# Three sample-token products with 128 columns of weights in a delta-rule decoder kernel

## The chip, the cores and the metric

One core of a Trainium2 chip runs the whole kernel in one launch. The metric is the device time of an execution in microseconds; the time of a kernel is the median of its runs.

## The reference, cut to what matters

The reference is one inference step of a hybrid decoder layer with 1088 tokens of 1024 features: 1024 tokens of a new sequence (the prompt) and 64 sample tokens, 8 sequences of 8 tokens each, that continue from stored states. One input projection gives the inputs of a pooling branch and of a gated delta branch with 8 heads of 128. The delta branch, for each head and each chunk of tokens, computes

```
u = w_v - w_k @ s            # w_v, w_k: solutions of a unit triangular system
o = qg @ s + (q @ k.T * decay) @ u
s = glast * s + kt.T @ u
```

For the prompt this runs over chunks with a state `s` that is carried on; for the sample tokens each sequence is one chunk of 8 with its own starting state `s0`. All 64 sample tokens of a head fit in one 64x64 matrix that is block-diagonal with blocks of 8. The change touches only products of these 64 sample tokens. After the branches come two output projections (`pa`, `pb`), a merge by gates, a last projection (`wo`) and a layer norm.

## The kernel before, in words

All big projections ("dense") have a weight tile of 128 output features as the stationary side and 1088 tokens, in column chunks of 364, 362 and 362, as the moving side. Each fp32 weight and activation is split into a high and a low part in fp32r (`wh`, `wl`, `hhi`, `hlo`), so that one output chunk is 24 matmuls. ScalarE makes `wh`, GpSimd subtracts it from the raw weight for `wl` (`wsplit`, line 336), a tile ahead of its use. The small fp32 products of the delta branch are single calls in the code that show as two passes each in the profile ("x2").

The order of instructions is written out by a planner inside the kernel. The main generator (`phaseD`, line 1731) yields after each dense matmul; helper generators (`aux`) wait for flags, or for estimated times, and put their instructions between the dense matmuls. `_Timed.g` (line 140) keeps an estimated clock of each engine: a GpSimd operation with two inputs costs 0.17 + n/400 us, another one 0.17 + n/1050; a TensorE fp32 product costs n/550 us, a third of it when the output has 32 partitions, and half when it has 64 and n is 64. `bank("m", x, ...)` (line 290) lets a helper go on when TensorE's estimated time has reached the estimated completion of its inputs and of the last use of one of two PSUM banks. The estimate knows when an input was written; of the reuse of a buffer it knows nothing. On the chip every engine runs its own instructions in this order and waits on semaphores.

The delta phase runs for each head `h` three dense tiles (Q, V, ZB) in the main generator and, between them, these helpers:

- `pre` and `prep` (line 1459). `prep` copies the sample columns of key and query into `kq` on GpSimd, multiplies `kt.T @ q` for eight prompt chunks of 128 tokens, then for the 64 sample tokens: `kt[:, TP:T]`, 128 rows by 64 columns, is the stationary side, 64 query columns are the moving side. VectorE multiplies the result by the decay in `e2`.
- `recur` (line 1495), the chain over eight chunks of the prompt, with products between `S`, `ktr`, `ttm`, `r`, `uh`, `qg`.
- `samples` (line 1550). Sixteen narrow products with `s0` (32 weight columns each), two VectorE steps that give `r` (tile `rs_`), then two products with the inverse `tt[:, TP:T]`, 64 columns, once for partitions 0 to 63 of the result and once for 64 to 127 (so the result `u` stands twice); ScalarE copies `u` and its high part, GpSimd the low part and the spread form `ux`; then four products of 32 columns and 64 rows with `pt` (tile `e2r`), each for 16 tokens, the 16 columns ahead of them being of no use; a transpose, and the new states.
- `vtoks` (line 1695) copies the sample part of `v` twice into `v2` on GpSimd and transposes it on TensorE.
- `post0`, `post1` (line 1651), the head norm; the last step issues the store to `d_yb`.

In the phase behind it (`phaseD7`, line 1795) `pa` tiles are computed until the flag of head 7's `post1` is set at the end of one; then buffers are exchanged and `yb` is loaded and split for the `pb` tiles.

In the profile all instructions have line L163, the one line of the helper that issues them, so groups are told apart by tile names: `psm<-us,e2r`, `psm<-rs_...,ttm` and `psm<-q,ktr` with 64 columns are the products that the change touches.

Of the kernel before, what the change touches and what calls it, by code (L numbers as in the profile page):

```python
# [9 lines left out]
F32 = mybir.dt.float32  # L10
# [8 lines left out]
TP = 1024  # L19
NB = 8  # L20
TS = 64
T = TP + TS
# [193 lines left out]
class _K:  # L216
# [1128 lines left out]
        self.flush()  # L1345


    def s128(self, nm):
        return self.X.tile([128, 128], F32, tag="u", name=nm, bufs=12)

    def loads(self, h):
        nc = self.nc
# [37 lines left out]
    def loads3(self, h):  # L1390
        nc, L = self.nc, self.L[h]
        L["s0"] = self.t("s0", shape=(128, 8, 128))
        nc.sync.dma_start(out=L["s0"], in_=self.A["s0"][h])

    def bc(self, ap, h, c0, n, p0, p1, w):
        return ap[p0:p1, c0:c0 + n, h].unsqueeze(2).to_broadcast([p1 - p0, n, w])
# [62 lines left out]
    def prep(self, h):  # L1459
        nc = self.nc  # L1460
        L = self.L[h]
        q = L["q"] = self.q[h]
        kt, e2 = L["kt"], L["e2"]
        kq = L["kq"] = self.s128("kq")
        gx = lambda ap: ap.rearrange("p (g x i) -> p g x i", x=2, i=16)
        gi = lambda ap: ap[:, TP:T].rearrange("p (g i) -> p g i", i=16)
        for x, src in enumerate((kt, q)):
            nc.gpsimd.tensor_copy(gx(kq)[:, :, x, :], gi(src))
        qg = L["qg"]

        def scaled():
            yield from self.on(qg)
            for i in range(4):
                cs = slice(256 * i, 256 * i + 256)
                nc.gpsimd.tensor_tensor(out=qg[:, cs], in0=qg[:, cs], in1=q[:, cs], op=ALU.mult)
                yield 3
            self.flags.add(("qg", h))
        self.aux(scaled())
        for g in range(2):
            ps = yield from self.bank("m", kt, q, e2)  # L1480
            for c in range(4):
                cs = slice(128 * (4 * g + c), 128 * (4 * g + c) + 128)
                nc.tensor.matmul(ps[:, 128 * c:128 * c + 128], kt[:, cs], q[:, cs], start=True, stop=True)
            gs = slice(512 * g, 512 * g + 512)
            nc.vector.tensor_tensor(out=e2[:, gs], in0=ps, in1=e2[:, gs], op=ALU.mult)
        ps = yield from self.bank("m")
        nc.tensor.matmul(ps[0:64, 0:64], kt[:, TP:T], q[:, TP:T], start=True, stop=True)
        nc.vector.tensor_tensor(out=e2[0:64, TP:T], in0=ps[0:64, 0:64], in1=e2[0:64, TP:T], op=ALU.mult)
        yield from self.until(("qg", h))
        for c0, n in CHUNKS:  # L1490
            cs = slice(c0, c0 + n)
            nc.scalar.activation(out=q[:, cs], in_=q[:, cs], func=AF.Square, scale=(RMS_EPS * 128.0) ** 0.5)
            yield 3
# [56 lines left out]
    def samples(self, h):  # L1550


        nc = self.nc
        V = nc.vector
        L = self.L[h]
        s0, kq, o, pt = L["s0"], L["kq"], L["qg"], L["e2"]
        ps = yield from self.bank("m", kq, s0)
        for j in range(2):
            for g in range(4):
                nc.tensor.matmul(ps[32 * g:32 * g + 32, 128 * j:128 * j + 128], kq[:, 32 * g:32 * g + 32],  # L1560
                                 s0[:, 2 * g + j, :], start=True, stop=True)
        r, u = self.s128("rs_"), self.s128("us")
        V.scalar_tensor_tensor(out=r, in0=ps[:, 0:128], scalar=self.cg[:, 0, h:h + 1], in1=L["vs"],
                               op0=ALU.mult, op1=ALU.add)
        V.scalar_tensor_tensor(out=r, in0=ps[:, 128:256], scalar=self.cg[:, 1, h:h + 1], in1=r,
                               op0=ALU.mult, op1=ALU.add)
        ps = yield from self.bank("m", r, L["tt"])
        for p0 in (0, 64):
            nc.tensor.matmul(ps[p0:p0 + 64, 0:128], L["tt"][:, TP:T], r, start=True, stop=True)
        self.acopy(u, ps[:, 0:128])  # L1570
        uh = self.X.tile([128, 128], F32R, tag="u", name="ush", bufs=12)
        ul = self.X.tile([128, 128], F32R, tag="u", name="usl", bufs=12)
        self.acopy(uh, u)
        nc.gpsimd.tensor_tensor(out=ul, in0=u, in1=uh.bitcast(F32), op=ALU.subtract)

        def spread(half):
            x = self.t("ux", F32R, (128, 2, 4, 128))
            for i, w in enumerate((uh, ul)):
                nc.gpsimd.tensor_tensor(
                    out=x[:, i], in0=w.bitcast(F32).unsqueeze(1).to_broadcast([128, 4, 128]),  # L1580
                    in1=self.cst[:, C_BM + 4 * half:C_BM + 4 * half + 4].unsqueeze(2)
                    .to_broadcast([128, 4, 128]), op=ALU.mult)
            return x
        ux = spread(0)
        ps = yield from self.bank("m", u, pt)
        for g in range(4):
            c0 = TP + 16 * g - 16
            nc.tensor.matmul(ps[32 * g:32 * g + 32, 0:128], pt[0:64, c0:c0 + 32], u[0:64],
                             start=True, stop=True)
        ot = self.s128("ot")  # L1590
        V.tensor_tensor(out=ot, in0=ps[:, 0:128], in1=r, op=ALU.add)
        ps = yield from self.bank("m", ot)
        nc.tensor.transpose(ps[:, 0:128], ot, self.ident)
        V.tensor_copy(o[:, TP:T].rearrange("p (g i) -> p g i", i=16),
                      ps[:, 0:128].rearrange("p (g x i) -> p g x i", x=2, i=16)[:, :, 1, :])
        self.aux(self.osq(L, slice(TP, T)))
        for half in range(2):
            ps = yield from self.bank("m", L["ks"], ux)
            for i in range(2):
                nc.tensor.matmul(ps, L["ks"], ux[:, i].rearrange("p b e -> p (b e)"),  # L1600
                                 start=(i == 0), stop=(i == 1))
            if half == 0:
                x1 = spread(1)
            for b in range(4):
                bb = 4 * half + b
                yield from self.free(4.0)
                V.scalar_tensor_tensor(out=s0[:, bb, :], in0=s0[:, bb, :], scalar=self.gls[:, bb, h:h + 1],
                                       in1=ps[:, 128 * b:128 * b + 128], op0=ALU.mult, op1=ALU.add)
                yield 1
            if half == 0:  # L1610
                ux = x1
        yield from self.on(s0)
        self.store(self.A["o_ds"][h], s0)
# [427 lines left out]
```

## Time and profile before

| | |
|---|---|
| median of 3 runs | 1293.39 us (1293.36 to 1293.54) |
| profiled execution | 1293.13 us |
| its span, first to last instruction | 1291.4 us |
| TensorE matmul (PE) busy | 1272.5 us, 99%, 8216 instructions |
| TensorE weight load (PEld) busy | 1215.8 us, 94%, 8216 |
| VectorE (DVE) | 796.1 us, 62%, 1383 |
| ScalarE (ACT) | 545.1 us, 42%, 1288 |
| GpSimd (POOL) | 640.0 us, 50%, 869 |

The profiled execution is 1.7 us longer than its span, which is the time around the first and the last instruction. Busy shares are averages over the whole span. A matmul's end is modelled and overlaps the start of the next, so the time that TensorE spends on an instruction is read from one start to the next, not from the durations. Timeline rows merge instructions of one kind that follow each other; a row of `x4` begins at the first one's start and lasts to the last one's end.

### The profile page before, as it was taken

To read this page: it belongs to the slowest core of one execution; us is meant where nothing else is said; L and a number is where in the kernel's file an instruction comes from. 1 tells how busy PE (TensorE), PEld (TensorE's weight loads), DVE (VectorE), ACT (ScalarE), POOL (GpSimd) and SP (SyncE) were. 2 spreads that over 40 slices of the span, in tenths; PEclk is the share of its full clock that TensorE was granted. 3 is DMA by queue.
4 is the path that set the end of the run, shared out by engine and by line. 5 is a ranking of instruction groups with operands and counts; after the bars stand their busy time and mean duration, and the time that the engine had idled before them with its cause. 6 is when DMAs were issued, how large, how long until landed. Compare 5 with 4: busy or idle time off the path is not lost. (4 is left out here: it accounts for less than half of the span.)

```text
span 1291.4 us, 21998 instructions
## 1 busy us (share of the span) xinstructions
PE 1272.5 (99%) x8216; PEld 1215.8 (94%) x8216; DVE 796.1 (62%) x1383; ACT 545.1 (42%) x1288; POOL 640.0 (50%) x869
## 2 busy tenths in 40 slices
PE   7999999999999999999999999999999999999996
PEld 5899999999999999999999999999999999999885
DVE  4465567899915999725656567565567443443367
ACT  3576685432354224443545455354464232231011
POOL 4446566644647457434555553554549422253124
PEclk9999999999999999999999999999999999999999
DMA  9334574424264222264332324323353385455123
GB/s 374 132 133 144 183 229 144 129 93 146 101 197 140 85 95 75 75 199 138 99 127 75 101 77 156 120 61 120 122 189 125 125 261 195 139 177 179 66 103 110
DMA packets 112746, 178.79 MB, mean 138 GB/s; under 512 B 57584, under 2 KB 76544, under 8 KB 111616
## 3 DMA queue, kind: packets, MB, share of 16 engines
q1 hardware_dynamic: 111424, 173.02, 41.2%
q0 software_dynamic: 736, 4.21, 1.2%
q8 instruction: 65, 1.06, 0.4%
q14 instruction: 41, 0.34, 0.1%
q10 hardware_dynamic: 480, 0.16, 0.1%
HBM read 127.69 MB, written 49.65 MB: 137 GB/s over the span
## 5 line engine op out<-in xcount | busy, mean ns | idle before, releaser
L163 PE MATMUL psd<-hlo,wh 128*128 128x364 f32 x1488 | 494.7, 332 | 0.0
L163 PE MATMUL psd<-hhi,wl 128*128 128x364 f32 x1488 | 494.6, 332 | 0.0
L163 PE MATMUL psd<-hhi,wh 128*128 128x364 f32 x1488 | 494.5, 332 | 0.0
L163 POOL TENSOR_TENSOR wl<-wr,wh 128x256 fp32r<-128x256 f32 x328 | 289.8, 895 | 349.1 <-ACT wh L163 337.2
L163 PEld LDWEIGHTS psd<-hhi,wh 128*128 128x128 f32 x1488 | 280.6, 189 | 3.2 <-issue 1.7
L163 PEld LDWEIGHTS psd<-hlo,wh 128*128 128x128 f32 x1488 | 280.9, 189 | 2.1 <-issue 1.3
L163 PEld LDWEIGHTS psd<-hhi,wl 128*128 128x128 f32 x1488 | 280.7, 189 | 1.8 <-issue 1.2
L163 DVE SCALAR_TENSOR_TENSOR cacc<-cext,small,cacc 128x362 f32<-128x362 f32 (+2 forms) x216 | 153.4, 722 | 67.6 <-ACT cacc L163 63.2
L163 ACT ACTIVATE wh<-wr 128x256 fp32r<-128x256 f32 x328 | 122.7, 407 | 28.2 <-PE psd L163 17.7
L163 DVE TENSOR_TENSOR P<-Tm,L 128x2048 f32<-128x2048 f32 (+35 forms) x136 | 111.5, 820 | 4.6
L163 DVE TENSOR_REDUCE Tm<-P 128x64 f32<-128x2048 f32 (+38 forms) x136 | 87.6, 644 | 4.2
L163 ACT ACT_TABLE_LOAD x65 | 83.4, 1283 | 5.5 <-issue 2.4
L163 ACT ACTIVATE cext<-psd 128x364 f32<-128x364 f32 (+1 forms) x88 | 32.4, 394 | 83.1 <-PE psd L163 83.0
L163 POOL TENSOR_TENSOR q<-q,o 128x128 f32<-128x128 f32 (+1 forms) x72 | 33.6, 468 | 67.8 <-ACT o L163 64.2
L163 PE MATMUL psd<-yah,wh 128*128 128x362 f32 (+1 forms) x192 | 63.8, 332 | 0.0
L163 PE MATMUL psd<-yah,wl 128*128 128x362 f32 (+1 forms) x192 | 63.4, 330 | 0.0
L163 PE MATMUL psd<-yal,wh 128*128 128x362 f32 (+1 forms) x192 | 63.3, 330 | 0.0
L163 PE MATMUL psd<-ybh,wh 128*128 128x362 f32 (+1 forms) x192 | 63.0, 328 | 0.0
L163 PE MATMUL psd<-ybl,wh 128*128 128x362 f32 (+1 forms) x192 | 63.0, 328 | 0.0
L163 PE MATMUL psd<-ybh,wl 128*128 128x362 f32 (+1 forms) x192 | 62.6, 326 | 0.0
L163 ACT ACTIVATE sz<-psd 128x362 f32<-128x362 f32 (+1 forms) x48 | 22.5, 473 | 90.6 <-PE psd L163 90.6
L163 ACT ACTIVATE sg<-psd 128x362 f32<-128x362 f32 (+1 forms) x48 | 22.8, 474 | 83.7 <-PE psd L163 83.6
(290 smaller groups left out, 2203.5 us busy)
## 6 DMA issues: line engine op xcount, KB each, us to landing
wr<-win SPq DMA_DIRECT2D x64, 512.0 KB
wada<-wada SPq DMA_DIRECT2D x16, 512.0 KB
gcb<-d_gc SPq DMA_DIRECT2D x8, 576.0 KB
xt<-xT SPq DMA_DIRECT2D x8, 544.0 KB
d_ga<-sg SPq DMA_DIRECT2D x8, 544.0 KB
d_e<-e SPq DMA_DIRECT2D x8, 544.0 KB
d_k<-kt SPq DMA_DIRECT2D x8, 544.0 KB
d_ya<-ya SPq DMA_DIRECT2D x8, 544.0 KB
```

The source lines that it names most:

```text
L163: return f(*a, **kw)
```

## The change

One buffer of 128x128 (`w2`) is added, and three products get 128 columns of weights. In `prep`, GpSimd copies `kt[:, TP:T]` twice side by side into `kd`, and the product gives its 64 rows twice. In `samples`, GpSimd copies `tt[:, TP:T]` twice side by side into `td`, and one product gives what two gave. Then GpSimd clears `w`, copies the 64x64 sample part of `pt` into every second group of 16 columns of its upper half, and one product takes the place of four. `kd`, `td` and `w` use the one buffer in turn. The waits (`bank`) name the copies.

```diff
-    def s128(self, nm):
-        return self.X.tile([128, 128], F32, tag="u", name=nm, bufs=12)
+    def s128(self, nm, tag="u", bufs=12):
+        return self.X.tile([128, 128], F32, tag=tag, name=nm, bufs=bufs)
...
+    def twice(self, copy, out, in_):
+
+        copy(out.rearrange("p (a i) -> p a i", a=2), in_.unsqueeze(1).to_broadcast([128, 2, 64]))
...
         self.aux(scaled())
+        kd = self.s128("kd", "w2", 1)
+        self.twice(nc.gpsimd.tensor_copy, kd, kt[:, TP:T])
         for g in range(2):
...
-        ps = yield from self.bank("m")
-        nc.tensor.matmul(ps[0:64, 0:64], kt[:, TP:T], q[:, TP:T], start=True, stop=True)
+        ps = yield from self.bank("m", kd)
+        nc.tensor.matmul(ps[:, 0:64], kd, q[:, TP:T], start=True, stop=True)
...
+        td = self.s128("td", "w2", 1)
+        self.twice(nc.gpsimd.tensor_copy, td, L["tt"][:, TP:T])
         r, u = self.s128("rs_"), self.s128("us")
...
-        ps = yield from self.bank("m", r, L["tt"])
-        for p0 in (0, 64):
-            nc.tensor.matmul(ps[p0:p0 + 64, 0:128], L["tt"][:, TP:T], r, start=True, stop=True)
+        ps = yield from self.bank("m", r, td)
+        nc.tensor.matmul(ps[:, 0:128], td, r, start=True, stop=True)
+        w = self.s128("pw", "w2", 1)
+        nc.gpsimd.memset(w, 0.0)
+        nc.gpsimd.tensor_copy(w[0:64].rearrange("p (g x i) -> p g x i", x=2, i=16)[:, :, 1],
+                              pt[0:64, TP:T].rearrange("p (g i) -> p g i", i=16))
...
-        ps = yield from self.bank("m", u, pt)
-        for g in range(4):
-            c0 = TP + 16 * g - 16
-            nc.tensor.matmul(ps[32 * g:32 * g + 32, 0:128], pt[0:64, c0:c0 + 32], u[0:64],
-                             start=True, stop=True)
+        ps = yield from self.bank("m", u, w)
+        nc.tensor.matmul(ps[:, 0:128], w, u, start=True, stop=True)
```

## Rows read from the trace of the kernel before

**Rows 1.** The page's first part: engine, busy us, share of the span, instructions.
```profile
span 1291.4 us, 21998 instructions
PE 1272.5 (99%) x8216; PEld 1215.8 (94%) x8216; DVE 796.1 (62%) x1383; ACT 545.1 (42%) x1288; POOL 640.0 (50%) x869
```
**Rows 2.** Windows: stretch, length, busy us of PE, PEld, DVE, ACT, POOL, PEclk, DMA.
```profile
576.00:1015.00 439.00, 438.69 (x3231) 419.52 (x3230) 266.86 (x557) 208.58 (x584) 235.29 (x393) 1.00 0.37 118
```
**Rows 3.** Waits of the weight loads: who waited for whom, us, times, longest.
```profile
PEld psm L163 <- POOL v L163: 0.4, 1, 0.4
```
**Rows 4.** Timeline of PE, head 0, at `rs_`: start, us, instruction, count.
```profile
601.73 0.32 PE L163 MATMUL psd<-hlo,wh 128*128 128x362 f32 x1
601.98 0.44 PE L163 MATMUL psm<-rs__6116,ttm 128*64 128x128 f32 x4
602.35 0.49 PE L163 MATMUL psc<-uh,ktok 128*128 128x128 f32 x2
602.67 0.28 PE L163 MATMUL pso<-e2r,uh 128*128 128x128 f32 x1
```
**Rows 5.** Timeline of PE, head 0, at `us`.
```profile
603.23 0.32 PE L163 MATMUL psd<-hlo,wh 128*128 128x362 f32 x1
603.49 0.42 PE L163 MATMUL psm<-us,e2r 64*32 64x128 f32 x8
603.84 0.49 PE L163 MATMUL psc<-S,ktr 128*128 128x128 f32 x2
604.08 0.41 PE L163 MATMUL psd<-hhi,wl 128*128 128x362 f32 x1
```
**Rows 6.** Timeline of PE, head 1, at the end of `prep`'s products.
```profile
642.38 0.98 PE L163 MATMUL psm<-q,ktr 128*128 128x128 f32 x7
...
643.56 0.33 PE L163 MATMUL psd<-hhi,wl 128*128 128x362 f32 x1
```
**Rows 7.** Timeline of PE, a wide fp32 product between dense matmuls.
```profile
662.05 0.33 PE L163 MATMUL psd<-hhi,wh 128*128 128x362 f32 x1
662.22 0.38 PE L163 MATMUL psc<-S,ktr 128*128 128x128 f32 x2
662.36 0.41 PE L163 MATMUL psd<-hlo,wh 128*128 128x362 f32 x1
662.61 0.33 PE L163 MATMUL psd<-hhi,wl 128*128 128x362 f32 x1
```
**Rows 8.** Timeline of PE, a wide product with 34 moving columns.
```profile
633.93 0.32 PE L163 MATMUL psd<-hhi,wh 128*128 128x362 f32 x1
634.09 0.30 PE L163 MATMUL psm<-st,cst 128*128 128x34 f32 x2
...
634.48 0.33 PE L163 MATMUL psd<-hhi,wl 128*128 128x362 f32 x1
```
**Rows 9.** Groups of GpSimd by form: count, busy us, mean ns, idle before.
```profile
L163 POOL TENSOR_TENSOR wl<-wr,wh 128x256 fp32r<-128x256 f32 x328 | 289.8, 895 | 349.1 <-ACT wh L163 337.2 <-DMA wr<-pa 7.2 <-issue 2.7
...
L163 POOL COPY v<-v 128x64 f32<-128x64 f32 x16 | 3.3, 234 | 0.0
...
L163 POOL COPY k<-ktr 128x128 f32<-128x128 f32 x8 | 2.6, 329 | 0.0
...
L163 POOL MEMSET gtmp<- 64x128 f32 x1 | 0.2, 195 | 0.0
```
**Rows 10.** Timeline of GpSimd, head 0, idle time ahead in brackets.
```profile
603.16 0.46 POOL L163 TENSOR_TENSOR usl<-us,ush 128x128 fp32r<-128x128 f32 x1 [3.40 <-ACT ush L163]
```
**Rows 11.** Timelines of SP, PE and DVE at the end of the delta phase.
```profile
1035.28 0.32 SPq L163 DMA_DIRECT2D d_yb<-e2r  x1
...
1036.95 0.33 PE L163 MATMUL psd<-yah,wh 128*128 128x364 f32 x1
...
1069.11 1.42 DVE L163 TENSOR_TENSOR ybl<-ybr,ybh 128x364 fp32r<-128x364 f32 x3
...
1084.23 0.33 PE L163 MATMUL psd<-ybh,wh 128*128 128x364 f32 x1
```

## The prediction, made before the changed kernel was run

> **What bounds the kernel now.** I read the busy shares first: TensorE's matmul row is busy for 1272.5 of the 1291.4 us of the span, 99%, and no other engine is near that [rows 1]. The reader should not stop there, because the ends of matmuls are modelled. So the second view is the stretch of the delta phase, 576 to 1015 us, in which all 24 changed products lie: TensorE 438.69 of 439.00 us, clock 1.00 (2.4 GHz) throughout, VectorE 267, ScalarE 209, GpSimd 235 us [rows 2]. The third is the waits: in the whole trace TensorE's weight loads waited once on GpSimd's copies of `v`, the nearest relative of what is added, for 0.4 us [rows 3]. TensorE is the limit, and it is fed. What can shorten the kernel is then a shorter sequence on TensorE itself, and such a gain is not hidden by anything: every stage after it is TensorE-bound too.
>
> The fourth view, the timeline, shows where TensorE loses time although it counts as busy: from one start to the next. A dense matmul of 362 columns occupies it for 0.165 us (662.05 to 662.22) [rows 7]. Around each narrow product there are holes that no such pitch explains.
>
> **Part 1: what a narrow product costs.** I take the time from the start of the dense matmul ahead to the first start behind that is back in step, and subtract what the other instructions between take in undisturbed places.
>
> - `us` with `e2r` (four products of 32 weight columns, eight passes): from the dense matmul at 603.23 to the next dense one at 604.08 are 0.85 us, with one wide product (`S,ktr`) between [rows 5]. A dense matmul and `S,ktr` alone take 0.31 us between the same two kinds of start (662.05 to 662.36) [rows 7]. The narrow one costs 0.54 us.
> - `rs_` with `ttm` (two of 64 columns, four passes): from 601.73 to 602.67 are 0.94 us, which hold one dense matmul (0.165) and one wide fp32 product (0.225, below) [rows 4]. The narrow one costs 0.55 us.
> - `q` with `ktr` (64 columns, two passes): from 642.38 to 643.56 are 1.18 us, which hold seven passes of this name and one dense matmul [rows 6]. Five of the seven are the wide passes of the product ahead, at 0.11 us each by half the price of a wide product; 1.18 - 0.56 - 0.165 leaves 0.455 us.
>
> The other seven heads repeat these patterns; I read all 24 and found them within 0.02 us of these once the kind of neighbour is allowed for.
>
> **Part 2: what a product with 128 columns costs.** `S,ktr` between dense matmuls: 662.05 to 662.61 is 0.56 us, less two dense matmuls (0.33) is 0.23 us [rows 7]. With only 34 moving columns, `st,cst`: 633.93 to 634.48 is 0.55 us, less 0.33 is 0.22 us [rows 8]. So the width of the moving side hardly counts here, and the new `kd` product (64 moving columns) lies between two measured rows. I take 0.225 us for each of the three.
>
> Here a rule of the Trainium skill speaks against the change. Its page "TensorEngine Tiling (Array Packing)", section Theoretical Speedup, promises up to 2x for dimensions up to 64 and 4x up to 32, because tiles work side by side; by that the narrow forms should be the cheaper ones and the saving zero or negative. The same page, section Key Properties, says that a change of tiling mode drains TensorE. The rows decide for the second: eight narrow passes stand together in 0.42 us, hardly more than the 0.38 us of a wide product's two [rows 5, 7], and yet the sequence is 0.31 us longer. By the first rule alone the time would stay at 1293.4 us.
>
> **Part 3: the saving.** Per head 0.455 - 0.225 = 0.23 us, 0.55 - 0.225 = 0.325 us and 0.54 - 0.225 = 0.315 us, together 0.87 us; with eight heads 7.0 us. Ends of this term: if the wide form costs 0.235 and the narrow ones 0.02 us less each, 0.78 a head or 6.2 us; the other way 0.96 or 7.7 us. The narrow products that stay (the two rounds with `s0`, the `az` ones) keep their holes.
>
> **Part 4: what is added on GpSimd.** Per head: two copies of 128x128 at 0.33 us, a memset of 128x128 at about 0.20 us (the 64x128 one), a copy of 64x64 at about 0.23 us (the 128x64 one) [rows 9]: 1.09 us, or 8.7 us in all. GpSimd is idle for 204 of the 439 us [rows 2], so the work itself costs nothing as long as no product waits for it. If that cover is gone, the price is the lateness of the copy, one for one, because TensorE runs in order and the dense matmuls queue behind the waiting weight load. The cushions: `td` can be copied as soon as `samples` begins; GpSimd is idle for 3.40 us up to 603.16, so from 599.76 on, and the product stands at 601.98 [rows 4, 10], some 1.9 us after a copy would end. `w` has to wait for the end of the `td` product (one buffer), about 602.4; 0.43 us of memset and copy end about 602.9, and the product stands at 603.49 [rows 5, 9]. `kd` is issued at the head of `prep`, behind the two `kq` copies, and its product comes after eight wide passes. GpSimd's next work there (`usl`, 603.16) needs ScalarE's `ush` anyway, so the wait of the memset for TensorE holds nothing up [rows 10].
>
> The new waits are not in this trace. Bounds: none, or one 0.895 us subtraction of `wl` ahead of every one of the 24 copies, 21.5 us [rows 9]; the nearest row is the single wait of 0.4 us over eight `v2` transposes, which were likewise made to wait for GpSimd copies just issued [rows 3], so 1.2 us for 24. As the new copies have more lead than those, I take 0.2 us. Below nothing is excluded: a wait cannot save time.
>
> **Part 5: order.** The planner prices TensorE, and its prices for the three products fall, so later work is issued at slightly other places between the dense matmuls. TensorE has almost no idle time to gain or lose by this in the phase (0.31 us) [rows 2]. For small new waits I leave 2.5 us either way. The sum against the profiled execution: 1293.13 - 7.0 + 0.2 = 1286.3 us; the median of the runs is 0.26 us above the profiled execution, so 1286.6 us.
>
> **Rivals.**
>
> *A, a late copy becomes TensorE's wait (slower).* The planner does not know that the three copies share one buffer, and it prices the subtraction of `wl` below what it takes. If copies queue behind `wl` each time, TensorE stands: at full price 1293.4 - 7.0 + 21.5 = 1307.9 us. It cancels the saving from 0.29 us of mean wait per product on, and is told from no change from 0.40 us on. Against it: GpSimd's idle 46% of the phase and the cushions above. Chance 0.06.
>
> *B, the tail takes another shape.* The phase after this one computes `pa` tiles until head 7's last step is issued, and loads `yb` only then. That issue (1035.28) comes 1.7 us ahead of the start of the next `pa` tile (1036.95) [rows 11]. If it slips past, one more `pa` tile is done first, which costs TensorE nothing, but `yb` arrives a tile later, 11.8 us by the pitch of these tiles (four from 1036.95 to 1084.23). Its last splits end at 1070.5 and the first use is at 1084.23, so 13.7 us of slack shrink to about 2 us: a cost of 0 to 3 us, 1286.6 to 1289.6 us. Chance 0.08.
>
> *C, the holes stay.* If the lost time does not go with the width, only the busy time of the products themselves changes: 0.44 to 0.38 and 0.42 to 0.38 us [rows 4, 5, 7], 0.1 us a head, 0.8 us in all: 1292.6 us. The same holds if the new products land next to the narrow ones that stay. For it: these rows don't show the same product in both forms. Against it: wide products with all sorts of operands cost the same 0.22 to 0.23 us. Chance 0.08. The speed-up rule of the Trainium skill's page "TensorEngine Tiling (Array Packing)" would end here as well.
>
> **How the numbers follow.** The forecast holds 0.78 (1284.0 to 1289.5 us by its own terms). The range 1284.0 to 1290.5 us takes in B and leaves out A, C and a little at both ends. This kernel's times repeat so closely that 0.2%, 2.6 us, tells a change from none: faster (below 1290.8 us) 0.86, same 0.09 (C and a mild A), slower 0.05 (the rest of A).
>
> **What would show it.** In the changed kernel TensorE should have 64 matmuls fewer (eight a head: two of four for `rs_`, six of eight for `us`), 8152, and GpSimd 32 instructions more, 901. The starts around the three products should keep the step of rows 7. The phase from 576 us to the first `pa` tile should be some 6 to 7 us shorter, and the stages ahead of it and behind it as long as before. Wrong would be: waits of weight loads on GpSimd beyond 1 us in sum (A), a fifth `pa` tile ahead of the `yb` loads with a gap at the first `pb` tile (B), or pitches around the new products that still exceed 0.45 us (C).

## The result, and the profile after

The changed kernel takes 1285.74 us (median of 4 runs, 1284.99 to 1285.92) against 1293.38 us before: a ratio of 0.9943, 95% interval 0.9931 to 0.9955, and below the 1290.8 us that the prediction set as the bound for faster. Measured again with the experiments it took 1286.53 us against 1293.09 us, ratio 0.9949 (0.9936 to 0.9961). The profiled execution took 1284.99 us, 1.8 us of it outside its span. Its first lines answer to [rows 1]: 64 matmuls fewer, 32 GpSimd instructions more, as counted.

```profile
span 1283.2 us, 21911 instructions
PE 1262.6 (98%) x8152; PEld 1215.2 (95%) x8152; DVE 803.0 (63%) x1383; ACT 545.0 (42%) x1288; POOL 650.2 (51%) x901
```

Where the time went is read from the windows of both kernels, cut at the same instructions: the first and the third dense tile behind the start, the first dense tile of the delta phase, the first `pb` tile, the end. Columns as in [rows 2]. First before:

```profile
51.39:88.83 37.44, 37.10 (x227) 36.51 (x226) 19.36 (x41) 25.50 (x52) 12.63 (x24) 0.95 0.17 62
88.83:562.32 473.49, 473.49 (x2921) 466.42 (x2921) 350.62 (x473) 221.97 (x435) 270.47 (x307) 1.00 0.44 137
562.32:1084.23 521.91, 521.60 (x3738) 502.43 (x3737) 301.20 (x619) 236.58 (x649) 260.88 (x428) 1.00 0.41 130
1084.23:1291.36 207.12, 196.66 (x1033) 177.83 (x1032) 102.34 (x187) 40.02 (x102) 69.59 (x78) 0.99 0.41 135
```

and after:

```profile
51.57:87.37 35.80, 35.47 (x226) 34.87 (x226) 19.80 (x41) 25.80 (x53) 12.82 (x23) 1.00 0.19 66
87.37:560.86 473.49, 473.49 (x2921) 466.42 (x2920) 350.16 (x473) 221.84 (x434) 270.59 (x306) 1.00 0.44 137
560.86:1076.09 515.23, 514.89 (x3673) 503.92 (x3673) 306.44 (x619) 236.11 (x649) 270.43 (x460) 1.00 0.41 132
1076.09:1283.18 207.09, 196.66 (x1033) 177.85 (x1032) 103.19 (x187) 40.02 (x102) 69.80 (x78) 0.98 0.41 135
```

The stretch that holds the change, 562 to 1084 us, is 6.68 us shorter. The stretch ahead of it and the one behind it are the same to 0.03 us. Another 1.64 us of the two spans' difference lie in the first window, which the change does not touch: there the mean granted clock is 0.95 before and 1.00 after. A narrower window of the two kernels shows it:

```profile
67.00:70.30 3.30, 3.30 (x13) 3.30 (x12) 1.42 (x6) 3.24 (x7) 0.10 (x1) 0.50 0.00 0
```
```profile
67.00:70.30 3.30, 3.30 (x23) 3.30 (x22) 1.24 (x4) 3.26 (x6) 0.00 (x0) 1.00 0.00 0
```

Before, the clock was at its lower level (1.2 GHz) for these 3.3 us and 13 matmuls had part in them; after, it was at 2.4 GHz with 23. The experiments' kernels, which are alike in this window, show both cases too (it lasts 37.43 us in `td_only`, 35.80 us in `kd_only` and in `narrow_twice`), so this belongs to the execution and not to the change. The spread of the kernel before, 1291.73 to 1294.89 us over 33 runs beside the experiments, is of the size of two such steps. The change itself is worth 6.7 us, and a single profile would have shown 8.2.

The timeline of TensorE after, in head 0, at the places of [rows 4, 5] and behind the products of `prep`, which [rows 6] show for head 1:

```profile
584.06 0.83 PE L163 MATMUL psm<-q,ktr 128*128 128x128 f32 x6
584.73 0.33 PE L163 MATMUL psm<-q,kd 128*128 128x64 f32 x2
584.87 0.41 PE L163 MATMUL psd<-hhi,wh 128*128 128x362 f32 x1
585.12 0.33 PE L163 MATMUL psd<-hlo,wh 128*128 128x362 f32 x1
...
600.01 0.33 PE L163 MATMUL psd<-hlo,wh 128*128 128x362 f32 x1
600.18 0.38 PE L163 MATMUL psm<-rs__6120,td 128*128 128x128 f32 x2
600.40 0.39 PE L163 MATMUL psc<-uh,ktok 128*128 128x128 f32 x2
600.62 0.39 PE L163 MATMUL pso<-e2r,uh 128*128 128x128 f32 x2
...
601.18 0.32 PE L163 MATMUL psd<-hlo,wh 128*128 128x362 f32 x1
601.35 0.38 PE L163 MATMUL psm<-us,pw 128*128 128x128 f32 x2
601.56 0.39 PE L163 MATMUL psc<-S,ktr 128*128 128x128 f32 x2
601.71 0.41 PE L163 MATMUL psd<-hhi,wl 128*128 128x362 f32 x1
```

The holes are gone. At `rs_`, from dense to the second product behind, 0.61 us (600.01 to 600.62) where [rows 4] have 0.94: 0.33 less. At `us`, 0.53 us (601.18 to 601.71) where [rows 5] have 0.85: 0.32 less. `kd` takes 0.39 - 0.165 = 0.225 us (584.73 to 585.12), where the narrow one took 0.455. The trace has the same differences, to 0.02 us, at all 24 places, once the kind of neighbour is allowed for.

GpSimd after: the group of the added memset (columns as in [rows 9]), and then the timeline at the place of [rows 10]:

```profile
L163 POOL MEMSET pw<- 128x128 f32 x8 | 1.6, 204 | 9.0 <-PE psm L163 9.0
```
```profile
597.46 0.29 POOL L163 COPY td<-ttm 128x128 f32<-128x128 f32 x1
...
600.63 0.20 POOL L163 MEMSET pw<- 128x128 f32 x1 [2.46 <-PE psm L163]
600.89 0.23 POOL L163 COPY pw<-e2r 64x64 f32<-64x64 f32 x1
601.30 0.46 POOL L163 TENSOR_TENSOR usl<-us,ush 128x128 fp32r<-128x128 f32 x1 [0.17 <-ACT ush L163]
```

The memset does wait for TensorE's product on the shared buffer, 9.0 us in sum over seven of the eight heads, but behind it stands `usl`, which waits for ScalarE still. The copy into `w` ends at 601.12, 0.23 us ahead of its product (601.35). In the list of what TensorE's weight loads waited for in this stretch GpSimd does not appear.

The tail, to be compared with [rows 11], has the last store of `yb` 1.67 us ahead of the next `pa` tile:

```profile
1027.14 0.32 SPq L163 DMA_DIRECT2D d_yb<-e2r  x1
...
1028.81 0.33 PE L163 MATMUL psd<-yah,wh 128*128 128x364 f32 x1
```

### The profile page after: what moved, and what is told of

Same layout as the page of the kernel before. It is cut to its first block, busy times and chain, and to the rows that moved or that the text cites. A ratio compares the mean times of both kernels' runs of the same rounds, so it can differ in the third digit from the quotient of the medians.

```text
span 1283.2 us, 21911 instructions
## 1 busy us (share of the span) xinstructions
PE 1262.6 (98%) x8152; PEld 1215.2 (95%) x8152; DVE 803.0 (63%) x1383; ACT 545.0 (42%) x1288; POOL 650.2 (51%) x901
## 5 line engine op out<-in xcount | busy, mean ns | idle before, releaser
L163 DVE SCALAR_TENSOR_TENSOR cacc<-cext,small,cacc 128x362 f32<-128x362 f32 (+2 forms) x216 | 158.4, 745 | 55.8 <-ACT cacc L163 51.6
L163 ACT ACTIVATE sz<-psd 128x362 f32<-128x362 f32 (+1 forms) x48 | 22.5, 473 | 83.8 <-PE psd L163 83.7
```

The lines of the kernel that those rows point to most:

```text
L163: return f(*a, **kw)
```

## The experiments

A product's form is its rows by columns of weights, and a visit is a run of passes in another form between passes of 128 by 128. Theory W: the loss lies in the holes ahead of and behind a narrow group, and is paid once per visit. Rival N: the gain goes with the number of matmuls. Rival G: the copies cost something that the sum hides. The table has the median, the median of the kernel before that was run beside it, and from the profile the stretch from the first dense tile of the delta phase to the first `pb` tile with the part of it in which TensorE was not busy. (Where an expectation speaks of 510.1 and 503.4 us it counts from the second tile.)

| run | median us | before | stretch us | not busy us |
|---|---|---|---|---|
| before | | | 521.91 | 0.31 |
| changed kernel | 1285.74 | 1293.38 | 515.23 | 0.34 |
| after_again | 1286.53 | 1293.09 | 515.16 | 0.36 |
| kd_only | 1291.73 | 1293.13 | 520.23 | 0.89 |
| td_only | 1291.37 | 1293.13 | 520.44 | 1.28 |
| w_only | 1289.74 | 1293.13 | 519.42 | 0.32 |
| copies_narrow | 1292.49 | 1293.13 | 521.55 | 0.15 |
| copies_twice | 1284.54 | 1293.09 | 513.95 | 0.00 |
| narrow_twice | 1294.30 | 1293.09 | 523.01 | 0.14 |
| w_rows64 | 1288.99 | 1292.57 | 518.39 | 0.36 |
| kk_wide | 1288.87 | 1293.09 | 515.51 | 0.55 |
| kk_early | 1289.46 | 1292.57 | 515.22 | 0.33 |
| kk_six | 1283.71 | 1292.42 | 514.96 | 0.36 |

**One product at a time.** Each kernel is the changed one with two of the three products, and their copies, put back. For `kd_only`, the part for the inverse:

```diff
-        td = self.s128("td", "w2", 1)
-        self.twice(nc.gpsimd.tensor_copy, td, L["tt"][:, TP:T])
...
-        ps = yield from self.bank("m", r, td)
-        nc.tensor.matmul(ps[:, 0:128], td, r, start=True, stop=True)
+        ps = yield from self.bank("m", r, L["tt"])
+        for p0 in (0, 64):
+            nc.tensor.matmul(ps[p0:p0 + 64, 0:128], L["tt"][:, TP:T], r, start=True, stop=True)
...
```

> Only the product of key and query has 128 columns of weights; the other two are narrow as before. Theory W (the loss lies in the narrow form: holes ahead of and behind a narrow group, whatever its number of matmuls): 8 x 0.23 us = 1.8 us faster than before, 1291.6 us. Rival N (the gain goes with the number of matmuls that fall away, eight a head for about 7 us, so 0.11 us each): this product has two passes before and after, so 0.0 us, 1293.4 us.

> Only the product with the inverse has 128 columns of weights. Theory W: 8 x 0.325 us = 2.6 us faster than before, 1290.8 us. Rival N: two matmuls fewer a head, 8 x 2 x 0.11 = 1.8 us, 1291.6 us.

> Only the product of the decayed scores and u has 128 columns of weights. Theory W: 8 x 0.315 us = 2.5 us faster than before, 1290.9 us. Rival N: six matmuls fewer a head, 8 x 6 x 0.11 = 5.3 us, 1288.1 us.

The ratios are 0.9988 (0.9980 to 0.9997), 0.9990 (0.9981 to 0.9999) and 0.9978 (0.9969 to 0.9986); the stretches are 1.68, 1.47 and 2.49 us shorter. N is refuted at both ends: `kd`, which loses no matmul, gains, and `w`, which loses six a head, gains 2.5 and not 5.3 us. The `td` kernel falls short of the 2.6 us because TensorE stood elsewhere. Its timeline, of TensorE:

```profile
974.02 0.32 PE L163 MATMUL psd<-hhi,wl 128*128 128x362 f32 x1
...
975.23 0.43 PE L163 MATMUL psd<-yah,wh 128*128 128x364 f32 x1 [0.89 <-ACT sz L163]
...
1002.65 0.49 PE L163 MATMUL psc<-r,ttm 128*128 128x128 f32 x2 [0.39 <-DVE r L163]
```

Two waits of 0.89 and 0.39 us, at the first `pa` tile and in the chain of head 7, make up its 1.28 us not busy, 0.97 more than before; with them added back the saving is 2.44 us. `kd_only` has the first of the two as well; with its 0.58 us added back it saves 2.26 us, more than the 1.8 us of theory W. The changed kernel, which holds the same `td`, has neither wait at this size, so they seem to come from the order that the planner writes and not from the product. Without the added idle time the three savings sum to 7.2 us, against 6.7 us of the changed kernel, so the size of each from its own kernel is sure to about half a microsecond only.

**The copies alone, and twice.** `copies_narrow` has all copies, waits and the one buffer, and reads them in the old forms; `copies_twice` is the changed kernel with each added GpSimd instruction issued twice; the edits for `td`, and likewise for the other two:

```diff
-        nc.tensor.matmul(ps[:, 0:128], td, r, start=True, stop=True)
+        for p0 in (0, 64):
+            nc.tensor.matmul(ps[p0:p0 + 64, 0:128], td[:, 0:64], r, start=True, stop=True)
```
```diff
         self.twice(nc.gpsimd.tensor_copy, td, L["tt"][:, TP:T])
+        self.twice(nc.gpsimd.tensor_copy, td, L["tt"][:, TP:T])
```

> All of GpSimd's copies, the one buffer and the waits of the changed kernel, but the three products read them in their narrow forms, with the matmuls of before. Theory W: copies and waits are covered, within 0.3 us of before, 1293.4 us, and the pitches around the three products as before. Rival G (the copies cost TensorE time, and the wide form gains more than the sum says): 1 us or more slower than before, with weight loads that wait for GpSimd.

> The changed kernel with every one of the added GpSimd instructions issued twice (8.7 us more of GpSimd work). Theory W: covered, within 0.3 us of the changed kernel. Rival G: the copies' time shows, from 0.4 us a head at the last product (memset and copy once more in a chain with 0.6 us of lead), 3.4 us, up to all 8.7 us.

The windows of the stretch, first of `copies_narrow`, then of `copies_twice`:

```profile
561.58:1083.13 521.55, 521.40 (x3737) 502.26 (x3737) 307.13 (x619) 237.24 (x649) 270.51 (x460) 1.00 0.41 130
```
```profile
561.35:1075.30 513.95, 513.95 (x3673) 503.94 (x3673) 313.97 (x619) 234.36 (x649) 290.62 (x492) 1.00 0.42 132
```

With 9.6 us more of GpSimd work (270.51 against 260.88) the old products take the old time, 0.36 us less; ratio 0.9998 (0.9989 to 1.0007). With 20 us more (290.62 against 270.43; some 8 us are the doubled instructions, the rest lies in other work of GpSimd) the new ones take no longer either. G is refuted. This does not show room for late copies, though: the planner prices the extra ones and moves the product. In head 0 it stands 1.72 us behind the one with the inverse, where the changed kernel has 1.17 (600.18 to 601.35):

```profile
600.67 0.38 PE L163 MATMUL psm<-rs__6122,td 128*128 128x128 f32 x2
...
602.39 0.38 PE L163 MATMUL psm<-us,pw 128*128 128x128 f32 x2
```

But both theories missed `copies_twice`: it is faster than the changed kernel, by 1.28 us in the stretch and 2.0 us in the median on the same chip. More work on GpSimd is no reason for that; what else differs is the order. Of the gain 0.34 us is the idle time that the changed kernel has, half of it at a product in head 3 and half at the start of the second `pa` tile:

```profile
776.38 0.44 PE L163 MATMUL psm<-cst,ktr 128*128 128x128 f32 x2 [0.17 <-DVE ktok L163]
...
981.12 0.32 PE L163 MATMUL psd<-yah,wl 128*128 128x362 f32 x1
981.61 0.41 PE L163 MATMUL psd<-yah,wh 128*128 128x364 f32 x1 [0.17 <-DVE sga L163]
```

(At the `pa` tile 0.49 us from start to start where 0.165 is the rule.) Where the other 0.9 us come from stays open. It is hardly the narrow groups that stay: they make 24 visits in both kernels, which take 22.7 and 22.5 us in all from the dense matmul ahead to the first start behind.

**The narrow group twice.** The kernel before, with the four products of `us` issued twice in a row.

```diff
-        for g in range(4):
+        for g in (0, 1, 2, 3, 0, 1, 2, 3):
```

> The kernel before, with the four narrow products of u issued twice in a row (the second time over the same result). Theory W: the holes are paid once, and eight more passes cost what sixteen narrow passes with s0 take beyond eight with u in the trace of before, 0.57 - 0.35 = 0.22 us a head: 1.8 us slower than before, 1295.2 us. Rival N: the narrow group costs its 0.54 us again, 4.3 us slower, 1297.7 us.

```profile
602.48 0.32 PE L163 MATMUL psd<-hlo,wh 128*128 128x362 f32 x1
602.73 0.64 PE L163 MATMUL psm<-us,e2r 64*32 64x128 f32 x16
603.30 0.49 PE L163 MATMUL psc<-S,ktr 128*128 128x128 f32 x2
603.54 0.41 PE L163 MATMUL psd<-hhi,wl 128*128 128x362 f32 x1
```

The timeline has the doubled group between the same neighbours: from 602.48 to 603.54 is 1.06 us where [rows 5] have 0.85: the second group costs 0.21 us, not another 0.54. Of eight narrow passes 0.21 us is work and some 0.33 us is the visit. The group takes the same time in all eight heads, which makes 8 x 0.21 = 1.7 us; the stretch is only 1.10 us longer, the ratio 1.0010 (1.0001 to 1.0019). Of the 0.6 us between them 0.17 is idle time that fell away; the rest stays open.

**Rows instead of columns.** The changed kernel with `w` cut to its upper 64 rows, 128 columns kept.

```diff
-        nc.tensor.matmul(ps[:, 0:128], w, u, start=True, stop=True)
+        nc.tensor.matmul(ps[:, 0:128], w[0:64], u[0:64], start=True, stop=True)
```

> The changed kernel, but the product with u uses 64 rows and 128 columns of weights (the lower 64 rows, which are zero, are left out, with the rows of u that they multiply). If only narrow columns cost the holes: 0.23 us a product, as the changed kernel. If any other form of the array than 128 rows by 128 columns costs them: two passes in a form of their own, 0.455 us by the product of key and query with 64 columns, 0.23 us more a head, 1.8 us slower than the changed kernel.

```profile
601.69 0.32 PE L163 MATMUL psd<-hlo,wh 128*128 128x362 f32 x1
601.95 0.48 PE L163 MATMUL psm<-us,pw 64*128 64x128 f32 x2
602.36 0.49 PE L163 MATMUL psc<-S,ktr 128*128 128x128 f32 x2
602.61 0.41 PE L163 MATMUL psd<-hhi,wl 128*128 128x362 f32 x1
```

The stretch is 3.16 us longer than in the changed kernel. From 601.69 to 602.61 is 0.92 us, less 0.31 us is 0.61 us for two passes: more than the eight narrow ones cost before. So 128 columns of weights are not enough, the product needs 128 rows too, and the zero rows of `w` earn their memset. Theory W has to speak of any form other than 128 by 128, and not of narrow columns. The size was underrated: I had taken 0.455 us from the 64-column product.

**One more product of the kind.** In the phase ahead, the sample tokens' key-by-key product (`kk`) is narrow too. `kk_wide` gives it a GpSimd copy and 128 columns, `kk_early` issues the copy ahead of the store and of the wait for two buffers, `kk_six` leaves heads 3 and 7 narrow.

```diff
+        k2 = self.s128("kk2", "w2", 1)
+        self.twice(nc.gpsimd.tensor_copy, k2, kt[:, TP:T])
...
-        ps = yield from self.bank("m", kt)
-        nc.tensor.matmul(ps[0:64, 0:64], kt[:, TP:T], kt[:, TP:T], start=True, stop=True)
+        ps = yield from self.bank("m", k2)
+        nc.tensor.matmul(ps[:, 0:64], k2, kt[:, TP:T], start=True, stop=True)
```

> The changed kernel once more, for comparison on the same chip as the next three. Theory W: 7.0 us faster than before, 1286.4 us; the stretch from the first dense tile of the delta phase to the first pb tile 6.7 us shorter in the profile (510.1 to 503.4 us), the rest as before.

> The changed kernel, and the same for the narrow key-by-key product of the sample tokens in the phase ahead (128 columns of weights, copied by GpSimd). Theory W: 8 x 0.23 us = 1.8 us faster than the changed kernel, 1283.9 us. Rival N: two passes before and after, no gain, 1285.7 us.

> As the earlier kernel with the wide key-by-key product, but GpSimd's copy is issued as soon as the key is ready, ahead of the store and of the wait for two free buffers. Theory W with the waits that the earlier run showed (a copy 1.7 us late, and one product held 2.4 us behind VectorE): the copy's wait goes; if VectorE's goes as well, 8 x 0.23 = 1.8 us faster than the changed kernel, 1284.2 us with the 1286.0 us of its runs so far; if VectorE's stays, with the clock's step behind it, 1286 to 1288 us. Rival N: the wide form gains nothing here, and what is left is the waits: not below 1286.0 us in either case, and the phase ahead of the delta phase not below 473.5 us from its third dense tile on.

> The kernel with the wide key-by-key product, but heads 3 and 7, whose product waited for GpSimd (1.7 us) and behind VectorE (2.4 us), keep the narrow form without a copy. Theory W (these two waits, and the clock's step after the second, are all that ate the gain): the stretch ahead of the delta phase is 6 x 0.23 = 1.4 us shorter than in the changed kernel, 472.1 us from its third dense tile on against 473.5, and the time 1.4 us below the changed kernel, 1284.7 us. Rival O (any new order in this stretch brings such waits, in other heads): they come back elsewhere, and the stretch is longer than 473.5 us.

The window from the third dense tile to the delta phase (473.49 us in the changed kernel), in `kk_wide`, `kk_early` and `kk_six`:

```profile
87.37:564.46 477.09, 473.59 (x2921) 468.31 (x2920) 355.55 (x472) 219.12 (x433) 277.92 (x314) 1.00 0.42 134
```
```profile
89.18:566.13 476.95, 473.62 (x2920) 468.33 (x2920) 355.64 (x472) 219.26 (x433) 277.45 (x314) 1.00 0.42 134
```
```profile
87.74:559.66 471.92, 471.92 (x2920) 466.62 (x2920) 354.23 (x473) 221.39 (x434) 269.23 (x312) 1.00 0.44 137
```

The first two lost 3.6 and 3.5 us there instead of gaining 1.8, and their medians missed what theory W expected (1288.87 us against 1283.9, 1289.46 us against 1284.2 to 1288). The timeline of `kk_wide` names the places:

```profile
148.31 0.32 PE L163 MATMUL psd<-hhi,wh 128*128 128x362 f32 x1
150.00 0.43 PE L163 MATMUL psm<-kt,kk 128*128 128x64 f32 x2 [1.37 <-POOL kk L163]
...
237.90 0.41 PE L163 MATMUL psm<-kt,kk 128*128 128x64 f32 x2 [2.12 <-DVE mt L163]
...
239.22 0.51 PE L163 MATMUL psd<-hhi,wh 128*128 128x364 f32 x1
239.52 0.51 PE L163 MATMUL psd<-hlo,wh 128*128 128x364 f32 x1
```

One product stood for a late GpSimd copy: the rival A of the prediction, met in another phase. Another stood for a PSUM bank that VectorE had not yet emptied, and behind that idle time the matmuls go 0.30 us apart. Its window has the clock at the lower level:

```profile
238.90:242.10 3.20, 3.20 (x12) 3.20 (x12) 3.20 (x3) 0.00 (x0) 3.20 (x2) 0.50 0.55 103
```

Issuing the copy earlier did not help: in `kk_early` GpSimd stands in that place 4.48 us for ScalarE's `wh`, works off the subtraction that is queued there, and only then copies.

```profile
149.51 1.53 POOL L163 TENSOR_TENSOR wl<-wr,wh 128x256 fp32r<-128x256 f32 x1 [4.48 <-ACT wh L163]
...
151.31 0.29 POOL L163 COPY kk<-kt 128x128 f32<-128x128 f32 x1
```

Leaving out the two heads did: 1.57 us shorter in that window, 1.4 expected, no step of the clock there, and 1283.71 us, ratio 0.9935 (0.9921 to 0.9949), the lowest median here, level with `copies_twice` (0.9937) within the noise. N, which allowed no gain here, and O are refuted for this edit.

## Why the prediction was right

- *TensorE is the limit, and a shorter sequence is not hidden.* Right: the stretches that the change does not touch kept their length to 0.03 us but for the clock's step.
- *Narrow against wide.* Predicted 0.23, 0.325 and 0.315 us a head; from start to start they measured 0.23, 0.33 and 0.32. The sum of 7.0 us stands against 6.68 us in the stretch. The 0.3 us between them are not idle time, of which the stretch has 0.31 us before and 0.34 after; where they went stays open.
- *The rule against the change.* The Trainium skill's "TensorEngine Tiling (Array Packing)", section Theoretical Speedup, promises up to 2x and 4x for small dimensions. For these groups as a whole it did not hold: eight passes of 64 by 32 cost 0.54 us, a wide product 0.225. Within a visit it does: the second eight passes of `narrow_twice` took 0.21 us, 0.026 us each, against 0.11 for a wide pass. The same page of the Trainium skill, section Key Properties, says that a change of tiling mode drains TensorE. The 0.33 us a visit in `narrow_twice` and the 0.61 us in `w_rows64` agree with that; they show the cost, not the drain itself.
- *GpSimd's work is covered.* Right: the 0.2 us for waits were not spent. The memset waited for the product with the inverse, as forecast (GpSimd stood idle for 2.46 us ahead of it in head 0), and held nothing up, because `usl` behind it had to wait for ScalarE anyway. The cushion of `w` was mis-sized: forecast some 0.6 us between the end of the copy and the product, measured 0.23. That it was enough is in part the planner's doing, which places the product by the price of the copy, as `copies_twice` shows.
- *Rivals.* A did not happen here, but `kk_wide` shows that it was a real danger: one late copy cost 1.4 us, six products' gain. B did not happen: the last store came 1.67 us ahead of the next `pa` tile, as before, and from there to the first `pb` tile it is 47.28 us in both kernels. C is refuted by the starts around the new products.
- *Order.* I left 2.5 us either way for it. The experiments show idle time of 0.4 to 0.9 us a place that comes and goes with edits elsewhere, and `copies_twice` differs by 1.28 us with the same products, so this term was needed, and it is larger than the terms of the waits that I could name.
- *The time.* 1286.6 us predicted, 1285.74 and 1286.53 us measured. The agreement to the last tenths is luck, since runs of one program differ by a step of the clock.

## What to carry to other kernels

In a stretch bound by TensorE read the starts, not the busy time: a lone product in another form than its neighbours costs two holes, and filling it up with copies or zeros to the neighbours' form was cheaper here by 0.23 to 0.33 us a product. The holes are paid once a visit, so expect less for each product where many share one; no run here fills up such a group. Check rows and columns both. Buy the operand's preparation on an engine that has idle time at that very place, and look through all heads for the one in which it does not.

## What was not expected of the hardware

- A product of 64 rows by 128 columns, two passes, costs 0.61 us between wide ones; eight passes of 64 by 32 cost 0.54, and two of 128 by 64 cost 0.455.
- One wait of 2.12 us by TensorE was followed, 1 us later, by 3.2 us at the lower clock (1.2 GHz): about 1.6 us more, as much as the gain of seven wide products. In `kk_early` the lower clock came 1.6 us behind the same wait. That the wait caused it is not shown: the step at 67 us in the kernel before came with TensorE busy throughout the 15 us ahead of it.
